# A gated DeltaNet chunk inverse rewritten: diagonal blocks of 64 by 64 x 64 products, and a block step to join them

## The chip, the cores and the metric

The kernel runs on one NeuronCore of one Trainium2 chip (trn2). The metric is the device time of one execution in microseconds (us). Three executions of the kernel before took 2860.15, 2866.6 and 2876.06 us; their median is 2866.6 us. One further execution was profiled; its rows are what this document reads.

## The reference, cut to what matters

Two transformer blocks of two layers each run one after the other on 256 tokens of width 1024, all in float32. The first block ends each layer with a mixture of experts. The second block's first layer has a bidirectional gated DeltaNet, for the 256 context tokens and for the 256 latent tokens. Per chunk of tokens it solves a unit lower triangular system:

```python
m = jnp.where(strict, jnp.einsum('nbhik,nbhjk->nbhij', k_beta, kc) * decay, 0.0)
a = jnp.eye(C, dtype=f32) + m
u = lax.linalg.triangular_solve(a, v_beta, left_side=True, lower=True, unit_diagonal=True)
w = lax.linalg.triangular_solve(a, k_beta * jnp.exp(gcum)[..., None],
                                left_side=True, lower=True, unit_diagonal=True)
```

The reference takes chunks of 64 tokens. The kernel takes chunks of 128, whose result is the same, and builds the inverse of `a` outright.

## The kernel before, in words

There are two streams of work. The stream S (tile names begin with m) carries the latent tokens: first the whole first block, then the second. The stream T (tile names begin with f) carries the context tokens through the second block's first layer. T's steps are handed out among S's mixtures of experts as fill: each S mark allows T a number of units (`FILL`, 14 per mark in the last mixture), and each `yield` of T says how many units its step used. A priority scheduler then puts every instruction of both streams into one fixed order per engine. An engine runs its instructions in that order; a tensor-engine (PE) instruction that waits holds up all behind it.

`gdn` (L1255) runs the DeltaNet for 2 chunks of 128 tokens, 2 directions and 4 heads. A pair (direction, chunk) is called a unit here. T works its four units one after the other (`groups` of one); S works two groups of two units. For each group there are three steps.

- `prepare` (L1276) builds the matrices of a unit, each of 128 partitions by 4 heads by 128: U (the strictly triangular system, transposed), the decayed scores `at`, the decayed keys `kt`, and room for X and Z.
- `level` (L1303), called 7 times (L1380), doubles the size of the inverted diagonal blocks: 1 to 2, 2 to 4, and so on to 128. X is the inverse so far, Z its transpose. Per level and unit there are up to three products (4 heads each, 128 x 128 by 128 x 128): pV = U'X, masked on VectorE (DVE) to the blocks of this level (L1311); pZ = V'Z (L1316); pX = Z'V (L1324). DVE then subtracts pX from X (L1325) and pZ from Z (L1326). Level 0 has no pX and the last level neither, so a unit takes 19 products and 20 DVE operations of 128 x 512 elements.
- `solve` (L1331) reads the state, multiplies by Z and updates output and state.

The hardware runs a float32 matmul as two instructions, so that a product of 4 heads is 8 MATMUL and 8 LDWEIGHTS in the trace. (The scheduler's order shows 4.)

Around `gdn` in each stream lie the projections before it, the 31-tap convolution `conv31` (L1083, mostly DVE at L1095, with a side chain on POOL), the output projection, and the feed-forward layers (tiles `mgu`, `fgu`, `facc`), which fill the gaps in PE's order. The tile `pada` (L997) is a modulation product from weights `adaw` loaded in threes; its matmuls stand among T's in PE's order. After the last mixture of experts comes a branch for experts that overflow (L911 and L912). It isn't taken.

Of the kernel before, what the change touches and what calls it, by code (L numbers as in the profile page):

```python
# [9 lines left out]
F32 = mybir.dt.float32  # L10
F32R = mybir.dt.float32r
BF = mybir.dt.bfloat16
I32 = mybir.dt.int32
AF = mybir.ActivationFunctionType
OP = mybir.AluOpType
# [328 lines left out]
class Kernel:  # L344
# [601 lines left out]
    def second_consts(self, S):  # L946
        nc, I, c = self.nc, self.I, self.consts
        self.gstrict = c.tile([128, 2, 128], F32, name="gstrict")
        self.gincl = c.tile([128, 2, 128], F32, name="gincl")
        nc.sync.dma_start(self.gstrict, I["c_gstrict"])  # L950
        nc.sync.dma_start(self.gincl, I["c_gincl"])
        self.gneg = c.tile([128, 2, 128], BF, name="gneg")
        gz = S.tmp([128, 2, 128], name="gz")
        nc.sync.dma_start(gz, I["c_gneg"])
        nc.vector.tensor_copy(self.gneg, gz)
        self.glev = c.tile([128, 2, 7, 128], BF, name="glev")
        for d in range(2):
            for q, n in ((0, 4), (4, 3)):
                gl = S.tmp([128, 4, 128], name="gl")
                nc.sync.dma_start(gl[:, :n], I["c_glev"][:, d, q:q + n])  # L960
                nc.vector.tensor_copy(self.glev[:, d, q:q + n], gl[:, :n])

        def row(name, src, n):
            t = c.tile([128, n], F32, name=name)
            nc.sync.dma_start(t, src[None, :].to_broadcast([128, n]))
            return t

        self.qkvw = c.tile([128, 12, 5], F32, name="qkvw")
        nc.sync.dma_start(self.qkvw, I["qkvw"])
        self.cfw = c.tile([128, 4, 31], F32, name="cfw")  # L970
        nc.sync.dma_start(self.cfw, I["cfw"])
        nc.vector.tensor_scalar(self.cfw, self.cfw, 0.5, None, op0=OP.mult)
        self.cfb = c.tile([128, 4], F32, name="cfb")
        nc.sync.dma_start(self.cfb, I["cfb"])
        self.onorm = row("onorm", I["gdn_out_norm_2"], 128)
        self.dtb = row("dtb", I["gdn_dt_bias_2"], 8)
        self.nega = row("nega", I["gdn_a_log_2"], 8)
        nc.scalar.activation(self.nega, self.nega, AF.Exp)
        nc.vector.tensor_scalar(self.nega, self.nega, -1.0, None, op0=OP.mult)
# [273 lines left out]
    def gdn(self, S, g, beta, krow, vrow, TT, ST, G, groups, first, need_state):  # L1253


        nc = self.nc
        V = nc.vector
        qT, kT = TT
        scale = 128.0 ** -0.5
        o = S.slab([128, 2, 4, 128], F32, "o")  # L1260
# [8 lines left out]
        egs = S.sm([128, 2, 2, 4], F32, "g_egs", 1)  # L1269
        V.tensor_scalar(egs, eg[:, 0], scale, None, op0=OP.mult)  # L1270
        yield 2.0
        idb = self.ident[:, None, :].to_broadcast([128, 4, 128])

        def bc(a):
            return a[:, :, None].to_broadcast([128, 4, 128])

        def prepare(d, c, i, kts):
            cs = slice(c * 128, (c + 1) * 128)
            A, B = G(), G()
            U, X, Z, at, kt = A[:, 0], A[:, 1], B[:, 0], B[:, 1], kts[:, i]  # L1280
            V.tensor_tensor(X, self.gstrict[:, d, None, :].to_broadcast([128, 4, 128]),
                            bc(g[:, c, 4 * d:4 * d + 4]), op=OP.mult)
            pd = S.ps([128, 4, 128], name="pD")
            for h in range(4):
                nc.tensor.matmul(pd[:, h], X[:, h], self.gincl[:, d], start=True, stop=False)
                nc.tensor.matmul(pd[:, h], self.identb, self.gneg[:, d], start=False, stop=True)
            E = S.tmp([128, 4, 128], name="E")
            nc.scalar.activation(E, pd, AF.Exp)
            p = S.ps([128, 4, 128], name="pkk")
            for h in range(4):  # L1290
                nc.tensor.matmul(p[:, h], kT[:, h, cs], kT[:, h, cs], start=True, stop=True)
            for h in range(4):
                V.scalar_tensor_tensor(U[:, h], p[:, h], beta[:, c, 4 * d + h:4 * d + h + 1], E[:, h],
                                       op0=OP.mult, op1=OP.mult)
            p = S.ps([128, 4, 128], name="pkq")
            for h in range(4):
                nc.tensor.matmul(p[:, h], kT[:, h, cs], qT[:, h, cs], start=True, stop=True)
            V.scalar_tensor_tensor(at, p, scale, E, op0=OP.mult, op1=OP.mult)
            last = 127 if d == 0 else 0
            V.tensor_tensor(kt, krow[:, c], E[:, :, last:last + 1].to_broadcast([128, 4, 128]), op=OP.mult)  # L1300
            return U, X, Z, at, kt

        def level(lev, batch):  # L1303

            V_ = []
            for (d, c), (U, X, Z, at, kt) in batch:
                pv = S.ps([128, 4, 128], name="pV")
                for h in range(4):
                    nc.tensor.matmul(pv[:, h], U[:, h], self.ident if lev == 0 else X[:, h], start=True, stop=True)
                v = S.tmp([128, 4, 128], name="Voff")  # L1310
                V.tensor_tensor(v, pv, self.glev[:, d, lev, None, :].to_broadcast([128, 4, 128]), op=OP.mult)  # L1311
                V_.append(v)
            for v, ((d, c), (U, X, Z, at, kt)) in zip(V_, batch):
                pz = S.ps([128, 4, 128], name="pZ")
                for h in range(4):
                    nc.tensor.matmul(pz[:, h], v[:, h], self.ident if lev == 0 else Z[:, h], start=True, stop=True)  # L1316
                if lev == 0:
                    V.tensor_tensor(X, idb, v, op=OP.subtract)
                    V.tensor_tensor(Z, idb, pz, op=OP.subtract)
                    continue  # L1320
                if lev < 6:
                    px = S.ps([128, 4, 128], name="pX")
                    for h in range(4):
                        nc.tensor.matmul(px[:, h], Z[:, h], v[:, h], start=True, stop=True)  # L1324
                    V.tensor_tensor(X, X, px, op=OP.subtract)  # L1325
                V.tensor_tensor(Z, Z, pz, op=OP.subtract)  # L1326

        done, seen = set(), set()

# [46 lines left out]
        for grp in groups:  # L1376
            kts = G()
            batch = [((d, c), prepare(d, c, i, kts)) for i, (d, c) in enumerate(grp)]
            yield 3.0 * len(grp)
            for lev in range(7):  # L1380
                level(lev, batch)
                yield 2.6 * len(grp)
            for (d, c), w in batch:
                solve(d, c, *w)
                yield 4.3
# [147 lines left out]
def prepare(x):  # L1533

    f = {k: np.asarray(v) for k, v in x.items()}
    o = {}
    c = np.ascontiguousarray
# [19 lines left out]
    q = f["w_q_up"].reshape(L, 3, 128, 8, 96)  # L1557
    q = np.concatenate([q, q[..., 80:96], q[..., 64:80]], -1)
# [37 lines left out]
    i = np.arange(128)  # L1596
# [17 lines left out]
    i, j = i[:, None], i[None, :]  # L1614
# [1 line left out]
    o["c_gincl"] = c(np.stack([i <= j, i >= j], 1).astype(f32))  # L1616
    o["c_gneg"] = c(np.stack([np.where(i <= j, 0, -30000.0), np.where(i >= j, 0, -30000.0)], 1).astype(f32))
    lev = []
    for s in range(7):
        w = 1 << s  # L1620
        lev.append(((i // (2 * w) == j // (2 * w)) & (i // w > j // w)).astype(f32))
    lev = np.stack(lev, 1)
    o["c_glev"] = c(np.stack([lev, lev.transpose(2, 1, 0)], 1))
    row = np.repeat(np.arange(4, dtype=f32), 64)
    col = np.tile(np.arange(64, dtype=f32), 4)
    inv = f32(10000.0) ** (-np.arange(32, dtype=f32) / f32(32))
# [125 lines left out]
```

## Time and profile before

| | |
|---|---|
| median of 3 runs | 2866.6 us (2860.15 to 2876.06) |
| the profiled execution's own time | 2867.61 us |
| its span in the trace | 2865.9 us |
| mean granted TensorE clock over the span | 0.972 |
| PE busy | 2663.8 us (93%) |
| DVE busy | 1663.0 us (58%) |
| ACT busy | 1009.6 us (35%) |
| POOL busy | 157.6 us (5%) |

How to read it: busy times are sums over the whole span, in which stages with different limits follow each other. The span in the trace is 1.7 us shorter than the execution's own time. A granted clock of 1.00 is 2.4 GHz and 0.50 is 1.2 GHz; a number between is a mean over the stretch.

### The profile page before, as it was taken

To read this page: it belongs to the slowest core of one execution; us is meant where nothing else is said; L and a number is where in the kernel's file an instruction comes from. 1 tells how busy PE (TensorE), PEld (TensorE's weight loads), DVE (VectorE), ACT (ScalarE), POOL (GpSimd) and SP (SyncE) were. 2 spreads that over 40 slices of the span, in tenths; PEclk is the share of its full clock that TensorE was granted. 3 is DMA by queue.
4 is the path that set the end of the run, shared out by engine and by line. 5 is a ranking of instruction groups with operands and counts; after the bars stand their busy time and mean duration, and the time that the engine had idled before them with its cause. 6 is when DMAs were issued, how large, how long until landed. Compare 5 with 4: busy or idle time off the path is not lost.

```text
span 2865.9 us, 44849 instructions
## 1 busy us (share of the span) xinstructions
PE 2663.8 (93%) x18016; PEld 2162.0 (75%) x18017; DVE 1663.0 (58%) x2895; ACT 1009.6 (35%) x1716; POOL 157.6 (5%) x183
## 2 busy tenths in 40 slices
PE   7999999888899998899999988999999999988998
PEld 6775555567755555788989986998989798965897
DVE  4752222548743474677687998734464434467766
ACT  3532223334533331123455213422333232244443
POOL 0000000010000120000000110000000000010000
PEclk9999999999999999999999999999999999999999
DMA  7659999873489997526655205654335743231564
GB/s 263 220 183 365 384 381 368 313 275 121 156 309 369 361 366 275 192 97 218 187 184 156 74 9 168 199 201 143 100 132 193 250 135 100 84 119 63 183 185 159
DMA packets 175720, 590.25 MB, mean 206 GB/s; under 512 B 29568, under 2 KB 32144, under 8 KB 175504
## 3 DMA queue, kind: packets, MB, share of 16 engines
q1 hardware_dynamic: 153504, 512.16, 51.3%
q10 hardware_dynamic: 18288, 66.59, 6.8%
q0 software_dynamic: 3712, 8.54, 0.9%
q8 instruction: 144, 2.36, 0.3%
q14 instruction: 72, 0.59, 0.1%
HBM read 572.39 MB, written 14.97 MB: 205 GB/s over the span
## 4 chain that ended last, share of the span: by engine, by line
PE 48%; DVE 6%; DMA 3%; issue 2%; POOL 1%; ACT 1%; SPq 0%; POOLq 0%; DVEq 0%; ACTq 0%
PE mgu L110 6%; PE mgu L111 6%; PE mgu L112 6%; PE macc L112 3%; PE macc L110 3%; PE macc L111 3%; PE fgu L111 3%; PE fgu L110 3%; PE fgu L112 3%; DMA adaw<-in_ada_w_dram 2%; PE facc L111 1%; PE facc L112 1%; PE facc L110 1%; PE pada L1035 1%; DVE mwl L104 1%
## 5 line engine op out<-in xcount | busy, mean ns | idle before, releaser
L104 DVE TENSOR_TENSOR mwl<-mraw,mwh 128x1024 fp32r<-128x1024 f32 x369 | 450.3, 1221 | 377.1 <-ACT mwh L103 376.7
L103 ACT ACTIVATE mwh<-mraw 128x1024 fp32r<-128x1024 f32 x369 | 390.8, 1059 | 695.4 <-PE mgu L111 151.9
L110 PE MATMUL mgu<-mxTh,mwh 128*128 128x256 f32 x1408 | 401.2, 285 | 2.6 <-ACT mxTh L170 2.6
L111 PE MATMUL mgu<-mxTl,mwh 128*128 128x256 f32 x1408 | 400.5, 285 | 2.4 <-DVE mxTl L171 2.3
L112 PE MATMUL mgu<-mxTh,mwl 128*128 128x256 f32 x1408 | 399.7, 284 | 0.0
L110 PEld LDWEIGHTS mgu<-mxTh,mwh 128*128 128x128 f32 x1408 | 270.1, 192 | 11.3 <-issue 4.4
L104 DVE TENSOR_TENSOR fwl<-fraw,fwh 128x1024 fp32r<-128x1024 f32 x127 | 154.1, 1220 | 210.0 <-ACT fwh L103 166.5
L111 PEld LDWEIGHTS mgu<-mxTl,mwh 128*128 128x128 f32 x1408 | 270.5, 192 | 3.7 <-DVE mxTl L171 3.4
L112 PEld LDWEIGHTS mgu<-mxTh,mwl 128*128 128x128 f32 x1408 | 270.4, 192 | 0.0
L807 PE MATMUL mpgu<-mraw,mxg 128*64 128x512 f32 x1024 | 239.4, 607 | 10.2 <-DMA mraw<-in_w_gu_dram 7.3
L103 ACT ACTIVATE fwh<-fraw 128x1024 fp32r<-128x1024 f32 x127 | 133.5, 1057 | 203.7 <-PE fgu L111 106.2
L807 PEld LDWEIGHTS mpgu<-mraw,mxg 128*64 128x64 f32 x1024 | 72.2, 139 | 136.4 <-issue 129.1
L111 PE MATMUL fgu<-fxTl,mwh 128*128 128x256 f32 x576 | 163.0, 283 | 0.0
L112 PE MATMUL fgu<-fxTh,mwl 128*128 128x256 f32 x576 | 162.7, 282 | 0.0
L110 PE MATMUL fgu<-fxTh,mwh 128*128 128x256 f32 x576 | 161.5, 280 | 0.0
L110 PE MATMUL fgu<-fxTh,fwh 128*128 128x256 f32 x480 | 140.7, 294 | 2.7 <-DVE fa L298 1.4
L112 PE MATMUL fgu<-fxTh,fwl 128*128 128x256 f32 x480 | 138.7, 291 | 4.0 <-DVE fwl L104 4.0
L111 PE MATMUL macc<-mwl,macth 128*128 128x512 f32 x352 | 138.3, 393 | 1.1 <-DVE mwl L104 1.1
L110 PE MATMUL macc<-mwh,macth 128*128 128x512 f32 x352 | 138.7, 394 | 0.0
L111 PE MATMUL fgu<-fxTl,fwh 128*128 128x256 f32 x480 | 138.0, 290 | 0.0
L112 PE MATMUL macc<-mwh,mactl 128*128 128x512 f32 x352 | 137.9, 393 | 0.0
L835 PE MATMUL mpd<-mraw,mea 128*64 128x512 f32 x512 | 119.5, 598 | 0.5 <-DMA mraw<-in_w_down_dram 0.3
(611 smaller groups left out, 5657.3 us busy)
## 6 DMA issues: line engine op xcount, KB each, us to landing
mraw<-in_w_gu_dram SPq DMA_DIRECT2D x256, 512.0 KB, 8.3
mraw<-in_ffn_gu_dram SPq DMA_DIRECT2D x176, 512.0 KB, 4.5
adaw<-in_ada_w_dram SPq DMA_DIRECT2D x144, 512.0 KB, 6.1
mraw<-in_w_down_dram SPq DMA_DIRECT2D x128, 512.0 KB, 9.5
mraw<-in_ffn_dn_dram SPq DMA_DIRECT2D x88, 512.0 KB, 4.1
fraw<-in_ffn_gu_dram ACTq DMA_DIRECT2D x60, 512.0 KB, 5.1
fraw<-in_ffn_dn_dram ACTq DMA_DIRECT2D x30, 512.0 KB, 6.1
mraw<-in_w_in_dram SPq DMA_DIRECT2D x26, 512.0 KB, 5.3
```

The lines of the kernel that those rows point to most:

```text
L103: nc.scalar.activation(h[:, :m], raw[:, o:o + m], AF.Copy)
L104: nc.vector.tensor_tensor(l[:, :m], raw[:, o:o + m], h.bitcast(F32)[:, :m], op=OP.subtract)
L110: self.kb.latest = nc.tensor.matmul(ps, a[0], b[0], start=start, stop=False)
L111: nc.tensor.matmul(ps, a[0], b[1], start=False, stop=False)
L112: nc.tensor.matmul(ps, a[1], b[0], start=False, stop=stop)
L807: return nc.tensor.matmul(p[64 * g:64 * g + 64], xg(k), raw, start=k == 0, stop=k == 7)
L835: return nc.tensor.matmul(acc[64 * c:64 * c + 64], at[:, f], raw, start=f == 0, stop=f == 3)
L1035: m = nc.tensor.matmul(p[32 * g:32 * g + 2], self.cond[:, k], raw[:, g * 256:(g + 1) * 256], start=k == 0, stop=k == 7)
```

## The change

The first six levels now invert only the two diagonal blocks of 64 of each unit. X and the transposed inverse lie side by side in the two 64-column halves of one tile (XZ), the two diagonal blocks above each other in the partitions. A product of 4 heads is 8 matmuls of 64 x 64 by 64 x 64 (`half_mm`), whose operands and outputs lie in partitions 0 to 63 for one block and 64 to 127 for the other, alternating; both write the same PSUM tile. DVE operations on them have 128 x 256 elements in place of 128 x 512. The seventh level is replaced by `join`: one off-diagonal 64 x 64 block per head by two products of 4 matmuls each, a DVE copy, a DVE multiplication by -1 and two ACT copies that put the diagonal blocks into the full Z, which POOL has set to zero in `prepare`. The masks shrink from 7 levels of 128 columns to 6 of 64. The units that T's steps report shrink too (1.8 for 2.6 per level, 1.5 for the join).

```diff
@@ second_consts
-        self.glev = c.tile([128, 2, 7, 128], BF, name="glev")
+        self.glev = c.tile([128, 2, 6, 64], BF, name="glev")
...
+        self.identh = c.tile([128, 64], F32, name="identh")
+        for b in range(2):
+            nc.vector.tensor_copy(self.identh[64 * b:64 * b + 64], self.ident[64 * b:64 * b + 64, 64 * b:64 * b + 64])
@@ gdn
-        idb = self.ident[:, None, :].to_broadcast([128, 4, 128])
+        idb = self.identh[:, None, :].to_broadcast([128, 4, 64])
@@ prepare
             U, X, Z, at, kt = A[:, 0], A[:, 1], B[:, 0], B[:, 1], kts[:, i]
+            nc.gpsimd.memset(Z, 0.0)
@@
+        halves = [slice(0, 64), slice(64, 128)]
+
+        def half_mm(p, a, b):
+
+            for h in range(4):
+                for s in halves:
+                    nc.tensor.matmul(p[s, h], a(h, s), b(h, s), start=True, stop=True)
+
         def level(lev, batch):
...
-            for (d, c), (U, X, Z, at, kt) in batch:
-                pv = S.ps([128, 4, 128], name="pV")
-                for h in range(4):
-                    nc.tensor.matmul(pv[:, h], U[:, h], self.ident if lev == 0 else X[:, h], start=True, stop=True)
-                v = S.tmp([128, 4, 128], name="Voff")
-                V.tensor_tensor(v, pv, self.glev[:, d, lev, None, :].to_broadcast([128, 4, 128]), op=OP.mult)
+            for (d, c), (U, XZ, Z, at, kt) in batch:
+                X = XZ[:, :, 0:64]
+                pv = S.ps([128, 4, 64], name="pV")
+                half_mm(pv, lambda h, s: U[s, h, s], lambda h, s: self.identh[s] if lev == 0 else X[s, h])
+                v = S.tmp([128, 4, 64], name="Voff")
+                V.tensor_tensor(v, pv, self.glev[:, d, lev, None, :].to_broadcast([128, 4, 64]), op=OP.mult)
                 V_.append(v)
...
-                if lev < 6:
-                    px = S.ps([128, 4, 128], name="pX")
-                    for h in range(4):
-                        nc.tensor.matmul(px[:, h], Z[:, h], v[:, h], start=True, stop=True)
-                    V.tensor_tensor(X, X, px, op=OP.subtract)
-                V.tensor_tensor(Z, Z, pz, op=OP.subtract)
+                px = S.ps([128, 4, 64], name="pX")
+                half_mm(px, lambda h, s: Zc[s, h], lambda h, s: v[s, h])
+                V.tensor_tensor(X, X, px, op=OP.subtract)
+                V.tensor_tensor(Zc, Zc, pz, op=OP.subtract)
+
+        def join(batch):
+
+            V_ = []
+            for (d, c), (U, XZ, Z, at, kt) in batch:
+                near, far = halves if d == 0 else halves[::-1]
+                p = S.ps([128, 4, 64], name="pV")
+                for h in range(4):
+                    nc.tensor.matmul(p[far, h], U[near, h, far], XZ[near, h, 0:64], start=True, stop=True)
+                v = S.tmp([128, 4, 64], name="Voff")
+                V.tensor_copy(v[far], p[far])
+                for s in halves:
+                    nc.scalar.activation(Z[s, :, s], XZ[s, :, 64:128], AF.Copy)
+                V_.append(v)
+            for v, ((d, c), (U, XZ, Z, at, kt)) in zip(V_, batch):
+                near, far = halves if d == 0 else halves[::-1]
+                p = S.ps([128, 4, 64], name="pZ")
+                for h in range(4):
+                    nc.tensor.matmul(p[near, h], v[far, h], XZ[far, h, 64:128], start=True, stop=True)
+                V.tensor_scalar(Z[near, :, far], p[near], -1.0, None, op0=OP.mult)
@@ the loop over groups
-            for lev in range(7):
+            for lev in range(6):
                 level(lev, batch)
-                yield 2.6 * len(grp)
+                yield 1.8 * len(grp)
+            join(batch)
+            yield 1.5 * len(grp)
```

The scheduler's order changes with it. On PE, in the first group of S's DeltaNet, a level of two units was this (mpV, mpZ, mpX are the PSUM tiles of the three products):

```order
L1309 MATMUL mpV<-mG 128x128 x8
L1316 MATMUL mpZ<-mG,mVoff 128x128 x4
L1324 MATMUL mpX<-mVoff,mG 128x128 x4
L1316 MATMUL mpZ<-mG,mVoff 128x128 x4
L1324 MATMUL mpX<-mVoff,mG 128x128 x4
```

and is now, with the same order of products and twice the matmuls, each of a quarter of the array:

```order
L1312 MATMUL mpV<-mG 64x64 x16
L1312 MATMUL mpZ<-mG,mVoff 64x64 x8
L1312 MATMUL mpX<-mVoff,mG 64x64 x8
L1312 MATMUL mpZ<-mG,mVoff 64x64 x8
L1312 MATMUL mpX<-mVoff,mG 64x64 x8
```

The second place is PE at the end of the last mixture of experts (mpgu, mpgT and mpd are the products of its last two experts), ahead of the branch L912. Before, with T's second unit (tiles f) beginning there:

```order
L835 MATMUL mpd<-mraw,mea 64x512 x8
L1309 MATMUL fpV<-ident,fG 128x128 x4
L1297 MATMUL fpkq<-fqkvT 128x128 x2
L1316 MATMUL fpZ<-ident,fVoff 128x128 x4
L1309 MATMUL fpV<-fG 128x128 x4
L997 MATMUL pada<-adaw,cond 2x256 x5
L911 TENSOR_LOAD mo_ci
```

and now:

```order
L1312 MATMUL fpZ<-fG,fVoff 64x64 x5
L835 MATMUL mpd<-mraw,mea 64x512 x8
L820 MATMUL mpgT<-ident,mgsb 128x128 x4
L1312 MATMUL fpZ<-fG,fVoff 64x64 x3
L1312 MATMUL fpX<-fVoff,fG 64x64 x8
L1312 MATMUL fpV<-fG 64x64 x8
L835 MATMUL mpd<-mraw,mea 64x512 x8
L1312 MATMUL fpZ<-fG,fVoff 64x64 x8
L1312 MATMUL fpX<-fVoff,fG 64x64 x8
L1312 MATMUL fpV<-fG 64x64 x8
L1312 MATMUL fpZ<-fG,fVoff 64x64 x8
L1312 MATMUL fpX<-fVoff,fG 64x64 x7
```

Before, T's second unit stood at its level 1 at the branch. Now it stands near the end of its level 4, and products of its levels 1 and 2 stand ahead of the last experts' products. The third place is DVE in the same S group (mcw is the convolution's accumulator). Before, from one mask to the next:

```order
L1311 TENSOR_TENSOR mVoff<-mpV,glev 128x512 x2
L1095 SCALAR_TENSOR_TENSOR mcw<-mu,cfw,mcw 128x249
L1095 SCALAR_TENSOR_TENSOR mcw<-mu,cfw,mcw 128x250
L1095 SCALAR_TENSOR_TENSOR mcw<-mu,cfw,mcw 128x251
L1325 TENSOR_TENSOR mG<-mG,mpX 128x512
L1326 TENSOR_TENSOR mG<-mG,mpZ 128x512
L1095 SCALAR_TENSOR_TENSOR mcw<-mu,cfw,mcw 128x252
L1325 TENSOR_TENSOR mG<-mG,mpX 128x512
L1326 TENSOR_TENSOR mG<-mG,mpZ 128x512
```

and now:

```order
L1323 TENSOR_TENSOR mVoff<-mpV,glev 128x256 x2
L1097 SCALAR_TENSOR_TENSOR mcw<-mu,cfw,mcw 128x246
L1097 SCALAR_TENSOR_TENSOR mcw<-mu,cfw,mcw 128x247
L1335 TENSOR_TENSOR mG<-mG,mpX 128x4x64
L1336 TENSOR_TENSOR mG<-mG,mpZ 128x4x64
L1097 SCALAR_TENSOR_TENSOR mcw<-mu,cfw,mcw 128x248
L1335 TENSOR_TENSOR mG<-mG,mpX 128x4x64
L1336 TENSOR_TENSOR mG<-mG,mpZ 128x4x64
```

One convolution step less stands in a level, and more of the convolution stands behind the last level.

## Rows read from the trace of the kernel before

**Rows 1.** The page: busy us of each engine (share of the span) xinstructions.

```profile
PE 2663.8 (93%) x18016; PEld 2162.0 (75%) x18017; DVE 1663.0 (58%) x2895; ACT 1009.6 (35%) x1716; POOL 157.6 (5%) x183
```

**Rows 2.** Windows: stretch in us, its length, busy of each engine, clock, DMA share, GB/s.

```profile
1130.00:1168.00 38.00, 26.86 (x180) 22.50 (x180) 26.03 (x40) 8.62 (x15) 2.04 (x2) 0.78 0.65 227
1168.00:1272.00 104.00, 99.65 (x893) 92.19 (x892) 66.50 (x114) 21.09 (x34) 5.31 (x6) 1.00 0.45 146
1598.00:1650.00 52.00, 48.09 (x401) 45.65 (x400) 50.18 (x95) 7.80 (x15) 6.79 (x9) 1.00 0.11 34
1650.00:1668.00 18.00, 11.93 (x88) 11.24 (x87) 16.32 (x32) 3.61 (x7) 4.59 (x6) 0.91 0.04 15
1668.00:1715.00 47.00, 44.19 (x356) 41.91 (x353) 43.84 (x80) 3.70 (x7) 5.14 (x7) 0.96 0.02 7
```

**Rows 3.** Timeline, S's DeltaNet: start us, us, engine line op out<-in xcount [idle before <-releaser].

```profile
1608.00 1.95 PE L1309 MATMUL mpV<-ident,mG 128*128 128x128 f32 x16
1611.81 1.87 PEld L1309 LDWEIGHTS mpV<-mG 128*128 128x128 f32 x16
1616.62 0.68 DVE L1325 TENSOR_TENSOR mG<-mG,mpX 128x512 f32<-128x512 f32 x1
1617.21 0.67 DVE L1326 TENSOR_TENSOR mG<-mG,mpZ 128x512 f32<-128x512 f32 x1
1623.87 1.06 PE L1309 MATMUL mpV<-mG 128*128 128x128 f32 x8
1630.17 2.10 PE L1309 MATMUL mpV<-mG 128*128 128x128 f32 x16
1646.13 1.06 PE L1338 MATMUL mpkS<-fstate,mqkvT 128*128 128x128 f32 x8
```

**Rows 4.** Groups by line, 1590 to 1745 us: busy, mean ns | idle before, releaser.

```profile
L1095 DVE SCALAR_TENSOR_TENSOR mcw<-mu,cfw,mcw 128x247 f32<-128x247 f32 (+14 forms) x86 | 43.0, 500 | 1.5
L1311 DVE TENSOR_TENSOR mVoff<-mpV,glev 128x512 f32<-128x512 f32 x28 | 19.2, 687 | 1.3 <-PE mpV L1309 0.6
```

**Rows 5.** Timeline of DVE: an operation of 128x256 and the next one.

```profile
1599.49 0.42 DVE L1236 SCALAR_TENSOR_TENSOR mu<-mgth,mpj 128x256 f32<-128x256 f32 x1
1599.82 0.47 DVE L1095 SCALAR_TENSOR_TENSOR mcw<-mu,cfw,mcw 128x247 f32<-128x247 f32 x1
```

**Rows 6.** Timeline: matmuls with 64 stationary columns, outputs in alternating partition halves.

```profile
109.34 0.42 PEld L625 LDWEIGHTS mpo<-mpTs,mv 128*64 128x64 f32 x8 [0.27 <-ACT mpTs L621]
109.34 0.66 PE L625 MATMUL mpo<-mpTs,mv 128*64 128x128 f32 x8
```

**Rows 7.** The instructions on tile mpo: duration ns min/median/max, first to last start, forms.

```profile
L625 PEld LDWEIGHTS mpo<-mpTs,mv x96: 132/137/231, 109.3 to 723.9; 128*64 128x64 f32 x96
L625 PE MATMUL mpo<-mpTs,mv x96: 272/273/476, 109.3 to 724.0; 128*64 128x128 f32 x96
```

**Rows 8.** The page: the experts' products, halves alternating, 512 moving columns.

```profile
L807 PE MATMUL mpgu<-mraw,mxg 128*64 128x512 f32 x1024 | 239.4, 607 | 10.2 <-DMA mraw<-in_w_gu_dram 7.3 <-issue 2.3 <-ACT mxg L774 0.4
```

**Rows 9.** Windows, tile mpaux alone (64 stationary, 2 moving columns, one half): PE, PEld, DVE.

```profile
212.50:213.50 1.00, 1.00 (x21) 1.00 (x19) 0.00 (x0) 1.00 0.92 336
...
214.50:215.50 1.00, 1.00 (x13) 1.00 (x12) 0.00 (x0) 0.52 0.99 348
```

**Rows 10.** Timeline of PE, end of the last mixture and T's second unit.

```profile
1109.07 1.06 PE L1368 MATMUL fpS<-fG 128*128 128x128 f32 x8
1110.05 3.65 PE L835 MATMUL mpd<-mraw,mea 128*64 128x512 f32 x16
1126.90 1.04 PE L997 MATMUL pada<-adaw,cond 128*2 128x256 f32 x14 [0.30 <-PEq L912]
1163.60 1.89 PE L997 MATMUL pada<-adaw,cond 128*2 128x256 f32 x16 [1.80 <-DMA adaw<-in_ada_w_dram]
1167.90 0.36 PE L112 MATMUL mgu<-mxTh,mwl 128*128 128x256 f32 x1
```

More of the change, by code (lines that the diff above doesn't have):

```diff
@@ L955, in second_consts @@
         nc.vector.tensor_copy(self.gneg, gz)
-        self.glev = c.tile([128, 2, 7, 128], BF, name="glev")
+        self.glev = c.tile([128, 2, 6, 64], BF, name="glev")
         for d in range(2):
[L958 to L961, printed above, removed]
+            gl = S.tmp([128, 6, 64], name="gl")
+            nc.sync.dma_start(gl, I["c_glev"][:, d])
+            nc.vector.tensor_copy(self.glev[:, d], gl)
+        self.identh = c.tile([128, 64], F32, name="identh")
+        for b in range(2):
+            nc.vector.tensor_copy(self.identh[64 * b:64 * b + 64], self.ident[64 * b:64 * b + 64, 64 * b:64 * b + 64])
         def row(name, src, n):
@@ L1312, in level @@
                 V_.append(v)
-            for v, ((d, c), (U, X, Z, at, kt)) in zip(V_, batch):
-                pz = S.ps([128, 4, 128], name="pZ")
-                for h in range(4):
-                    nc.tensor.matmul(pz[:, h], v[:, h], self.ident if lev == 0 else Z[:, h], start=True, stop=True)
+            for v, ((d, c), (U, XZ, Z, at, kt)) in zip(V_, batch):
+                X, Zc = XZ[:, :, 0:64], XZ[:, :, 64:128]
+                pz = S.ps([128, 4, 64], name="pZ")
+                half_mm(pz, lambda h, s: v[s, h], lambda h, s: self.identh[s] if lev == 0 else Zc[s, h])
@@ L1317, in level @@
                 if lev == 0:
                     V.tensor_tensor(X, idb, v, op=OP.subtract)
-                    V.tensor_tensor(Z, idb, pz, op=OP.subtract)
+                    V.tensor_tensor(Zc, idb, pz, op=OP.subtract)
                     continue
-                if lev < 6:
-                    px = S.ps([128, 4, 128], name="pX")
-                    for h in range(4):
-                        nc.tensor.matmul(px[:, h], Z[:, h], v[:, h], start=True, stop=True)
-                    V.tensor_tensor(X, X, px, op=OP.subtract)
@@ L1326, in level @@
-                V.tensor_tensor(Z, Z, pz, op=OP.subtract)
+                px = S.ps([128, 4, 64], name="pX")
[14 more added lines that the diff above has]
+                V_.append(v)
+            for v, ((d, c), (U, XZ, Z, at, kt)) in zip(V_, batch):
+                near, far = halves if d == 0 else halves[::-1]
[3 more added lines that the diff above has]
+                V.tensor_scalar(Z[near, :, far], p[near], -1.0, None, op0=OP.mult)
@@ L1618, in prepare @@
     lev = []
-    for s in range(7):
+    i, j = np.arange(64)[:, None], np.arange(64)[None, :]
+    for s in range(6):
         w = 1 << s
@@ L1622, in prepare @@
     lev = np.stack(lev, 1)
-    o["c_glev"] = c(np.stack([lev, lev.transpose(2, 1, 0)], 1))
+    lev = np.stack([lev, lev.transpose(2, 1, 0)], 1)
+    o["c_glev"] = c(np.concatenate([lev, lev]))
     row = np.repeat(np.arange(4, dtype=f32), 64)
```

## The prediction

> **What bounds the kernel now.** Read the page first: PE is busy 93% of the span and DVE 58% [rows 1]. That is an average, so the table of windows comes next, for the stretches in which the changed products run [rows 2]. T's DeltaNet lies beside the end of the last mixture of experts and the start of S's feed-forward layer. From 1130 to 1168 us PE is busy 26.9 of 38 us, since it waits for T's chain and for weights. From 1168 to 1272 us it is busy 99.7 of 104: there T's products compete with S's mgu, and every us of PE work removed is worth nearly a us. S's DeltaNet stands alone on its path from 1598 to 1715 us, and there DVE is the fuller engine: 50.2 of 52, 16.3 of 18, 43.8 of 47 us, with PE at 48.1, 11.9 and 44.2. So two engines are near their limit there, and both must be relieved. The groups by line say what fills DVE: 43.0 us of the convolution beside the level operations, 28 masks at 687 ns among them [rows 4]. The timeline gives the rhythm: the first group's levels begin at 1608.0 and its solve at 1646.1, 38.1 us, and a full level of two units takes 6.3 us (1623.87 to 1630.17) [rows 3].
>
> **PE, per unit.** Before: 16 weight loads of 128 columns start over 1.87 - 0.19 us, 0.112 us apart [rows 3]; a product is 8 of them, 0.9 us, and 19 products make 17.0 us. After: 17 products of 16 instructions each, and a join of 16 instructions, each product of it in one quarter of the array. Their pace p is the unknown, since nothing in the trace uses half the rows and half the columns. It is bounded by three neighbours. The expert products, in alternating column halves, take 239.4/1024 = 0.234 us per 512 columns [rows 8]; 128 columns alone take 0.112, which is 0.45 for 512, so that two halves do run side by side, into one PSUM tile. In proportion 64 columns would take 0.112/2/2 = 0.028 us: the lower end. The nearest row in size is mpo, 64 stationary columns in alternating halves: its loads start (0.42 - 0.137)/7 = 0.040 us apart and its matmuls, twice as long as the new ones, (0.66 - 0.273)/7 = 0.055 [rows 6, 7]. And mpaux, 64 stationary and 2 moving columns always in one half, issues 20 pairs in a us, 0.050 each, at full clock [rows 9]. I take 0.040, the load pace of mpo, because with moving columns halved the loads come to the front; 0.028 and 0.055 are the ends. A unit is then 17 x 16 x p + 16 x 0.050 = 272p + 0.8 = 11.7 us (8.4 to 15.8), a gain of 5.3 us.
>
> **DVE, per unit.** Two subtractions of 128x512 start 0.59 us apart [rows 3], a 128x256 operation and its successor 0.33 [rows 5]. 20 x 0.6 = 12.0 us become 18 x 0.33 + 2 x 0.33 = 6.6, so 5.4 us less; four units in S make 21.6.
>
> **S's DeltaNet.** A level of two units is 6 products: 48 x 0.112 = 5.4 us, and 6.3 in the trace, so 0.9 us of waits. After: 96p + 0.9 = 4.7 us at p = 0.040. A group is level 0 (4 products and waits, 3.5 us), five levels (23.5) and a join (1.6 of PE and some 1.4 of DVE in between), 30 us for 38.1: 8 us each, 16 for both. DVE sets a limit of its own: with the idle shares of [rows 2] kept, it allows its 21.6 us. The convolution now ends behind the levels, so I count **-17 us** (p = 0.028: levels of 3.6 us, where DVE's limit of -21 decides; 0.055: levels of 6.2, a group 38.3, 0).
>
> **T's DeltaNet.** Behind the branch at 1126.9 us [rows 10] stand before: 16 products of unit two (14.3 us) and units three and four (34.0), 48.3 us of PE. The order after has 3 products and a join of unit two there and the same two units: 3 x 16p + 0.8 + 2 x (272p + 0.8) = 592p + 2.4 = 26.1 us. That is 22.2 less: partly cheaper products, partly work moved ahead of the branch, where PE waits for expert weights. Two costs go against it. First, quarter-array products alternate with S's full-array mgu. Row fpS to mpd shows such a switch: the eighth fpS starts at 1109.07 + 7 x 0.112 = 1109.85 and mpd at 1110.05, 0.20 later and not 0.11, so 0.09 us each [rows 10]; four per level over twelve levels are 4.3 us. Second, T's levels 1 and 2 now stand ahead of the last experts' products, whose chain (product, mask, product, subtraction) costs them some 3 us that the weights' arrival doesn't cover. Net **-15 us** (0.028: 48.3 - 19.0 - 7.3 = -22; 0.055: 48.3 - 35.0 - 7.3 = -6). PE's idle time there, for adaw weights above all (1.8 us before one pada [rows 10]), I take as unchanged.
>
> The Trainium skill, TensorEngine Tiling (Array Packing), section Tiling Modes, says that a change of tiling mode drains the engine; the 0.09 us agree in direction, and it gives no price.
>
> Nothing is counted for the rest, with its cover: POOL's memset of Z (needed only by the join, six levels later; uncovered, one POOL step of the convolution's chain); the two ACT copies (beside the join's products; uncovered, under 1 us per unit); smaller masks at the start.
>
> **Sum.** 2867.6 (the profiled execution's own time, 1.0 above the median) - 17 - 15 = 2835.6, forecast **2835 us**, 1.1% faster. Changes under 0.5% (14 us) can't be told from none here.
>
> **Rivals.**
> - *The halves run fully side by side* (p = 0.028): 2867.6 - 21 - 22 = 2825. For it: the experts' 0.234 us. Against: those have eight times the columns behind each load.
> - *The halves don't overlap* (p = 0.055 or so): 2867.6 - 0 - 6 = 2862, no change. For it: every row with overlap uses all 128 rows, none shows two row halves side by side; 16 instructions of half the length then take what 8 took. The Trainium skill, TensorEngine Tiling (Array Packing), section Restrictions and Gotchas, speaks for this one: "Different row tiles cannot access same PSUM bank simultaneously". No run here shows it yet; the rows have column halves sharing a PSUM tile, at full overlap.
> - *The clock falls, and the kernel is slower.* The mpaux stretch has PE busy throughout, and yet the granted clock goes from 1.00 to 0.52, between the levels of 2.4 and 1.2 GHz, and the pace from 20 to 12.5 pairs per us, 0.080 us each [rows 9]. Quarter-array products keep PE busy with little work too, and in S's levels nothing else runs beside them. At p = 0.080 a level of two units is 8.6 us, a group 52 (+14 each, +28), and T's PE work behind the branch 49.8, with 7.3 of switches and delay +9: 2867.6 + 37 = 2905. It decides from p = 0.058, where S's two groups (544p + 8.4 us each, for 38.1) and T's 592p + 9.7 (for 48.3) together break even. Against it: 64 moving columns are far more than 2, and S's mgu runs among T's products.
> - *T's moved work holds the experts up*: if the last expert products wait 15 us rather than 3, and T's gain is gone, 2850; if S's convolution becomes the end of its stage as well, 2862.
>
> **Chances.** Forecast (p 0.034 to 0.047) 0.42; full overlap 0.20; no overlap 0.20; clock 0.12; hold-up 0.06. Faster by over 0.5% (under 2853): the first two, half of the hold-up, and a third of the no-overlap case, with p under 0.050: 0.72. Slower: 0.12. Same: 0.16. The range reaches from 2815, a little below full overlap since idle may close too, to 2864, and leaves out the clock and the tails.
>
> **What would show it.** Right: LDWEIGHTS and MATMUL of mpZ at 64x64 start about 0.04 us apart; full levels of S take 4.7 us; DVE's 128x256 masks last 0.42 us; the granted clock stays above 0.9 from 1598 us on; S's first uninterrupted mgu comes no later than 1168 us; T's last product comes well before 1272. Wrong: a pace of 0.055 or more, a clock near 0.5 in the levels or mpd of the last expert late behind T's products. If levels shrink as forecast and the time doesn't, the convolution on DVE, or pada's wait for adaw, took their place.

## The result and the profile after

Four runs of the changed kernel took 2827.94 to 2838.48 us, median 2831.64; four of the kernel before 2857.8 to 2876.06, median 2863.38. The ratio on record is 0.9879, 95% interval [0.9859, 0.9898] (the two medians as they stand give 0.9889): **1.2% faster**, where 2835 was forecast. The profiled execution after took 2827.94 us of its own, the lowest of its four, so that the two traces differ by 39.7 us and the medians by 31.7. The page after, for [rows 1]:

```profile
PE 2614.7 (93%) x19104; PEld 2105.0 (74%) x19105; DVE 1619.5 (57%) x2895; ACT 1017.0 (36%) x1732; POOL 164.0 (6%) x191
```

Two stretches hold the change. Both are cut at the same instructions in both traces. The *T stretch* goes from the 925th mpgu matmul (near the end of the last mixture) to the 409th macc matmul (S's first feed-forward layer behind it); T's DeltaNet lies in it. The *S stage* goes from the last mpj (S's projections ahead of its DeltaNet) to the 545th macc matmul, the 41st behind S's DeltaNet. The expectations below call its end the first macc; that one comes about 10 us earlier in every run (1744.3 before, 1707.4 after). Windows, columns as in [rows 2] (PE, PEld, DVE, ACT, POOL); before:

```profile
1050.50:1446.90 396.40, 365.29 (x2564) 305.92 (x2561) 255.05 (x387) 118.35 (x171) 20.54 (x23) 0.96 0.61 207
1596.40:1754.30 157.90, 135.99 (x1006) 125.33 (x1005) 142.91 (x263) 26.82 (x45) 19.28 (x24) 0.97 0.16 51
```

and after:

```profile
1056.10:1424.50 368.40, 339.56 (x3058) 275.53 (x3055) 235.46 (x387) 121.98 (x180) 23.75 (x28) 0.97 0.66 222
1575.80:1718.00 142.20, 117.40 (x1596) 103.72 (x1595) 130.07 (x273) 33.75 (x58) 20.00 (x26) 0.94 0.23 75
```

The T stretch lost 28.0 us, and PE's busy time there 25.7. The S stage lost 15.7, and DVE's busy time there 12.8; PE lost 18.6 and its idle time grew. That points to PE for the first; what bounds the second is taken up below. Together the two lost 43.7 us and the span 40.1, so that the other stretches grew by 3.6. Such differences lie within those of single traces: T's first fpV, ahead of which the change touches little but the masks, starts at 1032.5 to 1040.6 us in the profiled runs of this study.

The S stage didn't hold the same work before and after. T's feed-forward product facc (PE) has twice the matmuls in it; the tile facc alone, before and after:

```profile
1596.40:1754.30 157.90, 11.88 (x46) 8.26 (x46) 0.68 (x1) 0.00 (x0) 0.97 0.16 51
1575.80:1718.00 142.20, 24.22 (x92) 17.92 (x92) 2.05 (x3) 0.00 (x0) 0.94 0.23 75
```

The rhythm in S's first group, PE, for [rows 3]:

```profile
1591.70 0.63 PE L1312 MATMUL mpX<-mVoff,mG 64*64 64x64 f32 x16
1592.17 0.63 PE L1312 MATMUL mpZ<-mG,mVoff 64*64 64x64 f32 x16
1592.63 0.63 PE L1312 MATMUL mpX<-mVoff,mG 64*64 64x64 f32 x16
...
1601.91 0.68 PE L1312 MATMUL mpV<-mG 64*64 64x64 f32 x16 [0.27 <-DVE mG L1335]
...
1605.41 0.68 PE L1312 MATMUL mpV<-mG 64*64 64x64 f32 x16 [0.28 <-DVE mG L1335]
...
1610.75 1.16 PE L1368 MATMUL mpkS<-fstate,mqkvT 128*128 128x128 f32 x8
```

Products of 16 instructions start 0.467 us apart: **0.029 us per instruction**. A level of two units takes 3.5 us (1601.91 to 1605.41; 6.3 before), the group 23.6 (first mpV at 1587.11; 38.1 before). DVE beside it, for [rows 4, 5], at the 0.33 us pace that [rows 5] had promised:

```profile
1599.50 0.98 DVE L1097 SCALAR_TENSOR_TENSOR mcw<-mu,cfw,mcw 128x246 f32<-128x246 f32 x2
1600.40 0.41 DVE L1335 TENSOR_TENSOR mG<-mG,mpX 128x256 f32<-128x256 f32 x1
1600.73 0.42 DVE L1336 TENSOR_TENSOR mG<-mG,mpZ 128x256 f32<-128x256 f32 x1
```

But behind the last mpat (1677.16; the last product of S's solve) DVE still has eleven convolution steps to do, mixed with T's feed-forward (fa, factl, fwl):

```profile
1681.64 0.42 DVE L298 TENSOR_TENSOR fa<-fa,fgu 128x256 f32<-128x256 f32 x1
1681.97 0.99 DVE L1097 SCALAR_TENSOR_TENSOR mcw<-mu,cfw,mcw 128x251 f32<-128x251 f32 x2
1682.88 0.42 DVE L301 TENSOR_TENSOR factl<-fa,facth 128x256 fp32r<-128x256 f32 x1
1683.22 1.99 DVE L1097 SCALAR_TENSOR_TENSOR mcw<-mu,cfw,mcw 128x247 f32<-128x247 f32 x4
1685.22 1.22 DVE L104 TENSOR_TENSOR fwl<-fraw,fwh 128x1024 fp32r<-128x1024 f32 x1
```

The mtp that needs the convolution (mtp transposes the outputs of DeltaNet and convolution) starts at 1705.9: 27.9 us from the last mpat matmul's start (1678.0), 17.0 before (1725.0 to 1742.0). This distance, before and after:

```profile
1725.00:1742.00 17.00, 11.02 (x52) 8.24 (x51) 15.14 (x29) 5.73 (x10) 2.76 (x3) 1.00 0.51 186
1678.00:1705.90 27.90, 23.79 (x99) 18.04 (x99) 25.93 (x47) 9.64 (x13) 2.76 (x3) 0.94 0.35 102
```

S's solve ends 26.4 us earlier after the last mpj, and 10.9 of that are given back here, with 10.8 more of DVE's busy time: 5.0 us are the convolution's, 4.9 are T's fwl (6 for 2).

The end of the last mixture, PE, for [rows 10]:

```profile
1111.89 0.68 PE L1312 MATMUL fpV<-fG 64*64 64x64 f32 x16 [0.88 <-DVE fG L1330]
1113.60 0.90 PE L1312 MATMUL fpZ<-fG,fVoff 64*64 64x64 f32 x10 [1.03 <-DVE fVoff L1323]
1114.43 6.26 PE L807 MATMUL mpgu<-mraw,mxg 128*64 128x512 f32 x16
...
1123.74 3.65 PE L835 MATMUL mpd<-mraw,mea 128*64 128x512 f32 x16
...
1130.42 3.65 PE L835 MATMUL mpd<-mraw,mea 128*64 128x512 f32 x16 [0.31 <-DVE mea L825]
```

The last mpd starts 13.4 us later than before (1116.99), 7.9 of it since the 925th mpgu. T's products, which wait for DVE, stand ahead of the last experts, and the last mpgu runs at a fallen clock.

### The profile page after: what moved, and what is told of

Its sections match the earlier page's. It is cut to its first block, busy times and chain, and to the rows that moved or that the text cites. A ratio compares the mean times of both kernels' runs of the same rounds, so it can differ in the third digit from the quotient of the medians.

```text
span 2825.8 us, 47068 instructions
## 1 busy us (share of the span) xinstructions
PE 2614.7 (93%) x19104; PEld 2105.0 (74%) x19105; DVE 1619.5 (57%) x2895; ACT 1017.0 (36%) x1732; POOL 164.0 (6%) x191
```

## The experiments

All ratios are to runs of the kernel before on the same chip; stretch and stage are from one trace each.

| kernel | median us | ratio [95%] | T stretch | S stage |
|---|---|---|---|---|
| before | 2863.4 | 1 | 396.4 | 157.9 |
| the change | 2831.6 | 0.9879 [0.9859, 0.9898] | 368.4 | 142.2 |
| e1_halves_in_turn | 2839.0 | 0.9899 [0.9869, 0.9929] | 372.0 | 146.0 |
| e9_long_runs | 2846.2 | 0.9928 [0.9908, 0.9948] | 385.0 | 148.2 |
| e2_unit_two_held | 2828.4 | 0.9871 [0.9851, 0.9891] | 364.0 | 142.7 |
| e3_taps_to_pool | 2821.8 | 0.9849 [0.9829, 0.9870] | 375.0 | 132.4 |
| e10_13_taps_not_held | 2819.4 | 0.9835 [0.9815, 0.9854] | 373.0 | 132.1 |
| e5_held_13_taps | 2823.0 | 0.9846 [0.9825, 0.9867] | 369.8 | 136.2 |
| e6_held_16_taps | 2820.5 | 0.9835 [0.9812, 0.9858] | 368.2 | 134.4 |
| e7_t_alone | 2844.5 | 0.9923 [0.9898, 0.9948] | 371.5 | 157.8 |
| e4_s_alone | 2859.2 | 0.9974 [0.9960, 0.9987] | 396.8 | 142.7 |
| e8_s_alone_same_masks | 2854.9 | 0.9946 [0.9922, 0.9970] | 397.0 | 142.3 |

**Why 0.029? First, the halves in turn** (e1):

```diff
-            for h in range(4):
-                for s in halves:
+            for s in halves:
+                for h in range(4):
```

> The changed kernel, with the two halves of a product in turn: all four heads of the upper 64 partitions, then all four of the lower, in place of alternating. In the changed kernel a product of 16 instructions takes 0.467 us, 0.029 per instruction. Theory: neighbouring instructions on different halves run side by side, so without alternation a product takes 0.85 to 0.9 us, a full level of two units in S goes from 3.5 to about 6 us, S's stage loses 20 to 30 us and T's 8 to 15, total 2855 to 2875 us. Rival: an instruction of 64 x 64 costs 0.029 us by its size, whatever stands beside it: product 0.47 us, total 2828 to 2838 us.

Neither number came: the total is 1 us above the rival's range, and its interval overlaps the change's. The weight loads tell why:

```profile
1593.73 0.19 PEld L1312 LDWEIGHTS mpX<-mVoff,mG 64*64 64x64 f32 x2
1593.79 0.14 PEld L1312 LDWEIGHTS mpZ<-mG,mVoff 64*64 64x64 f32 x1
1593.84 0.14 PEld L1312 LDWEIGHTS mpX<-mVoff,mG 64*64 64x64 f32 x1
1593.84 0.14 PEld L1312 LDWEIGHTS mpZ<-mG,mVoff 64*64 64x64 f32 x1
1593.90 0.54 PEld L1312 LDWEIGHTS mpX<-mVoff,mG 64*64 64x64 f32 x11
```

The first loads of mpX, on the upper half, start among the last of mpZ, on the lower. Then mpX is alone: its 11 loads start (0.54 - 0.14)/10 = 0.040 apart on average, since they include its own change of halves; inside a half it is 0.05 to 0.06. Products start 0.57 us apart (mpX at 1593.73, the next mpZ at 1594.30). When mpX's first matmul starts, three of mpZ's last eight, which stand ahead of it in PE's order, are still to start (1593.78, 1593.84, 1593.90), and so runs of 8 overlap in part. Runs too long for that settle it (e9):

```diff
+        def half_mms(jobs):
+            for s in halves:
+                for p, a, b in jobs:
+                    for h in range(4):
+                        nc.tensor.matmul(p[s, h], a(h, s), b(h, s), start=True, stop=True)
...
-                half_mm(pz, lambda h, s: v[s, h], lambda h, s: self.identh[s] if lev == 0 else Zc[s, h])
...
-                half_mm(px, lambda h, s: Zc[s, h], lambda h, s: v[s, h])
...
+            half_mms(jobs)
```

> The changed kernel with longer runs on one half: first the upper half of all products that are ready together (pV of both units of S, then pZ and pX of both), then the lower half; 16 to 32 instructions in a run where e1 had 8. In e1 the instructions of one half start 0.055 us apart, but some 6 of the next half's start beside the last ones, so that a product took 0.577 us. Theory (two halves run side by side only where neighbouring instructions in PE's order alternate, and a half alone takes 0.055 each): 0.045 us or more per instruction over a level, S's full level 5 to 5.5 us (3.5 in the changed kernel), S's stage 146 to 156 us (142.2), the stretch from 1050 us to S's macc 380 to 392 us (368.5), total 2848 to 2865 us. Rival (PE runs ahead through any run of instructions, or an instruction costs 0.029 by its size): total 2828 to 2840 us.

```profile
1601.70 0.54 PEld L1312 LDWEIGHTS mpZ<-mG,mVoff 64*64 64x64 f32 x8 [0.19 <-DVE mVoff L1324]
1602.16 0.54 PEld L1312 LDWEIGHTS mpX<-mVoff,mG 64*64 64x64 f32 x8
1602.63 0.54 PEld L1312 LDWEIGHTS mpZ<-mG,mVoff 64*64 64x64 f32 x8
```

```profile
1050.20:1435.20 385.00, 364.61 (x3058) 301.56 (x3055) 236.59 (x387) 122.18 (x180) 24.03 (x28) 0.95 0.63 212
1585.10:1733.30 148.20, 128.12 (x1551) 118.81 (x1550) 124.92 (x263) 30.50 (x55) 19.67 (x26) 0.94 0.17 55
```

Eight loads of one half take 0.46 us: 0.058 each. Over S's levels the mean step is 0.051 (0.029 in the change, 0.039 in e1), a level takes 4.9 us, and the total is 2846, 2 us under the expected range. The theory holds: **the overlap comes from alternating neighbours**, and without it some 60% of the gain remain in S (9.7 of 15.7 us) and 40% in T (11.4 of 28.0). PE's time in the T stretch rose by 25.1 us and the stretch by 16.6. In S PE's rose by 10.7, and the stage by only 6.0: slower products give DVE time for the convolution, and mtp comes 19.1 us after the last mpat, not 27.9. T's fill in the stage is again as before the change (46 facc matmuls, 13.5 us, for 24.2 in the change), so that S's own products rose by some 21 us.

**What bounds S's stage? Taps moved from DVE to POOL** (a tap is one step of the convolution; e3, both streams; e10, S alone):

```diff
-            if k < 16 or k % 2 == 0:
+            if k < 10 or k % 2 == 0:
```

> The changed kernel, with 6 of the 23 convolution taps per channel block that DVE does moved to the side chain on ACT and POOL, which then has 13 of them. 24 taps of 0.40 us in S's stage, 9.6 us of DVE, go. Theory (the convolution on DVE ends S's stage: 12 of its taps stand behind the last mpat, and 28.7 us pass from the last mpat to the next mtp, where 17.9 passed before the change): that distance falls to 18 to 22 us, total 6 to 10 us less, 2821 to 2826. Rival (T's feed-forward fill on PE and its fwl on DVE set that distance): distance and total as they were, 2829 to 2838. A third: 13 POOL steps of about 0.85 us and as many ACT copies, 11 us per block, become the end: total up.

> The changed kernel with 13 of S's taps per block on POOL, T's taps as they were and unit two not held. Theory (S's stage is DVE's; holding unit two only moves work): S's stage 132 to 136 us, the stretch from 1050 us to S's macc 367 to 371 us as in the changed kernel, total 2819 to 2825 us, as good as e5. Rival (the held unit is worth some us of its own): total 2826 to 2832.

The edit moves fewer taps than these texts say. Even taps stay on DVE whatever the bound, so that of taps 10 to 15 only 11 and 13 go (15 was never there): 2 per block and not 6, 9 per block on POOL and not 13. The traces have 84 steps on DVE for 92, and 36 additions on POOL for 28. Of the 8 that moved, 6 are in the S stage, 3.1 us of DVE. Windows of e10:

```profile
1051.40:1424.40 373.00, 343.00 (x3059) 278.24 (x3055) 235.72 (x387) 122.05 (x180) 23.75 (x28) 0.96 0.65 219
1574.60:1706.70 132.10, 107.16 (x1563) 95.59 (x1562) 119.93 (x258) 33.91 (x60) 25.81 (x32) 0.96 0.21 66
```

The stage fell from 142.2 to 132.1 us, DVE's busy time in it from 130.07 to 119.93, and PE's as much, from 117.40 to 107.16. S's products are the same in both. So the equal fall doesn't single out DVE, and most of it isn't the taps': of DVE's 10.1 us, 6.0 are six steps of T's fln and 2.4 two of T's fwl, which the new order puts behind the stage, and of PE's 10.2, 7.9 are T's facc (59 matmuls for 92). By parts, up to the last mpat's start in the change and in e10, and from there to the mtp in e10:

```profile
1575.80:1678.00 102.20, 81.52 (x1439) 75.49 (x1438) 92.34 (x213) 18.86 (x39) 17.24 (x23) 0.93 0.11 33
1574.50:1673.10 98.60, 79.19 (x1440) 73.42 (x1439) 92.61 (x211) 22.18 (x43) 23.04 (x29) 0.97 0.12 35
1673.10:1695.60 22.50, 16.98 (x72) 12.98 (x71) 20.40 (x41) 7.54 (x11) 2.77 (x3) 0.92 0.55 186
```

Up to the last mpat 3.6 us went with DVE's work unchanged, at a higher granted clock. From there to mtp 5.4 went (6.7 in e3, which takes 21.2), with 5.5 of DVE's work and 6.8 of PE's. DVE is the fuller engine there in both (25.9 of 27.9 us and 20.4 of 22.5), which speaks for DVE as the limit of this last part. Shown is that with these taps on POOL the stage and the total are shorter. That DVE ends the stage is argued, not shown: T's feed-forward changed its place with the taps on both engines, and no run moves one without the other. e10 has the lowest median of the study, 0.4% under the change (e6 has the same ratio); the T stretch came 2 us above its expected range. That e3 met its range is luck, since it was worked out from three times the taps; e10's range went by e3's trace.

**Did T's moved work cost anything? Unit two held back** (e2; lastz is 0 times the last expert's output):

```diff
         for i, grp in enumerate(groups):
+            if S.name == "f" and i == 1:
+                while self.at < sum(len(m) for m in self.marks.values()):
+                    yield 1e3
+                gl = S.sm([128, 2, 8], F32, "g_l", 1)
+                V.tensor_copy(gl, g)
+                V.tensor_scalar(gl[0:64], g[0:64], self.lastz, None, op0=OP.add)
+                g = gl
```

> The changed kernel, with T's second unit made to wait for the last expert's output (its decay input has 0 times that output added), so that no product of unit two stands among the last experts' products. Theory (T's moved work holds the experts up): the last mpgu takes 3.65 us and not 6.26, at full clock, the last mpd starts 8 to 14 us earlier (about 1118 to 1124 for 1130.4), the branch and S's first mgu as much earlier; of unit two's own PE time (about 9 us) half lies in gaps before the first mgu and half beside S's mgu, so that the total falls by 3 to 9 us, to 2822 to 2829. Rival (the work only changes its place, and T's later end costs what the experts gain): the last mpd earlier all the same, total 2829 to 2838 or above.

```profile
1096.76 7.09 PE L808 MATMUL mpgu<-mraw,mxg 128*64 128x512 f32 x32
1105.48 3.65 PE L836 MATMUL mpd<-mraw,mea 128*64 128x512 f32 x16 [1.63 <-DMA mraw<-in_w_down_dram]
...
1111.74 3.65 PE L836 MATMUL mpd<-mraw,mea 128*64 128x512 f32 x16 [1.92 <-DVE mea L826]
...
1143.41 0.50 PE L110 MATMUL mgu<-mxTh,mwh 128*128 128x256 f32 x2 [0.35 <-ACT mxTh L170]
```

The experts end as the theory says: last mpd at 1111.74 for 1130.42, first mgu at 1143.4 for 1174.9. Counted from the 925th mpgu, the first mgu comes after 91.3 us, for 118.8 in the change and 109.3 before. Yet the T stretch is only 4.4 us shorter, and the total, though at the upper end of the theory's range, can't be told from the change's (ratio 0.9871): T's products now lie beside mgu. e5 against e10, the same pair with the taps moved, gives 369.8 for 373.0 in the stretch, and a total that is higher, not lower. So the hold-up is real and large where one looks at the experts, and PE's work behind it takes most of it back, as the rival has it.

Both together, and with more taps (e5, e6; `first` is 10 and 4 for S, 16 for T, which makes 9 and 12 taps per block on POOL in S):

```diff
-            if k < 16 or k % 2 == 0:
+            if k < first or k % 2 == 0:
```

> Unit two held back as in e2, and 13 taps per block on POOL as in e3, but in S alone (T keeps 7). Theory (both hold: the held unit shortens the stretch from the last experts to the middle of S's first feed-forward layer, and S's DeltaNet stage is DVE's): S's stage, last mpj to first macc, 132 to 134 us as in e3 (142.2 in the changed kernel), T's moved end as in e2; total 2815 to 2821 us, ratio to before 0.982 to 0.985, under the changed kernel and under e2 and e3. Rival (one of the two gains was drift of a run): total as e3's, 2821.8, or above.

> As e5, with 16 taps per block on POOL in S and 14 on DVE: 12 more taps of 0.40 us leave DVE, 4.8 us. Theory (DVE still ends S's stage): its length falls by another 4 to 5 us to 127 to 129 us. Rival (PE's chain of products and masks or the chain ACT-POOL of 16 x 0.85 = 13.6 us per block is the next limit): 131 to 134 us, no gain or a loss against e5.

e5 missed its range by 2 us, and its S stage by 2: its rival holds. Its distance to mtp is e10's, 22.5; but up to the last mpat it took 102.7 us at a granted clock of 0.92, e10 98.6 at 0.97, with the same work on DVE (92.8 and 92.6). So two traces of this part can differ by 4 us with the same work on DVE. In e6 the convolution is out of the way (mtp comes 16.9 us after the last mpat, as before the change), but the solve itself got longer, 106.2 us: rival again. What bounds it then wasn't tried.

**Do the parts add up?** One stream alone (e4 and e8 with `old` for T, e7 for S):

```diff
+        old = S.name == "f"
...
-            for lev in range(6):
-                level(lev, batch)
+            for lev in range(7 if old else 6):
+                (level_old if old else level)(lev, batch)
```

> The new inverse in S alone; T keeps seven full levels. By the places where the two traces stand, S's stage gave about 15 us (157.9 us from its last mpj to the first macc before, 142.2 after) and T's about 22, some of it drift of the run. Theory (the two gains add up): about 15 us less than before, ratio 0.9935 to 0.996. Rival (S's stage is held by its convolution and by T's fill and gains little by itself, or T's part is worth nothing by itself): ratio over 0.998, or under 0.990.

> e4 again (new inverse in S alone), without loading a second set of masks: they are cut from the old table. In e4 S's stage was 15 us shorter and the total only 6. Theory (e4 lost 5 to 7 us by loading and rounding both mask tables at its start: its products stand 5.2 us late at 79 us and 7.3 us late at 142 us against before): now 13 to 16 us under before, ratio 0.9943 to 0.9957. Rival (S's gain is given back behind its stage): ratio 0.997 to 0.999 again, and the loss lies behind 1760 us.

> The new inverse in T alone; S keeps seven full levels. Its masks are cut from the old table by four small copies, so that no mask is loaded twice. Theory (the gains add: in the traces the stretch from expert 14's products near 1050 us to S's macc near 1447 us is 396.4 us before and 368.4 after): that stretch 366 to 372, S's stage 157 to 159 as before, ratio to before 0.989 to 0.992. Rival (T's earlier end is worth less in the total, since it only moves S's wait): stretch 380 or more, ratio over 0.994.

In e4 the S stage was as expected (142.7) and the total, 0.26% under before, was short of it. The first mpq of e4, and of e8 behind it, 79.4 us before:

```profile
L110 PE MATMUL mpq<-mqlh,mwh x48: 279/283/472, 84.7 to 685.9; 128*128 128x256 f32 x48
```

```profile
L110 PE MATMUL mpq<-mqlh,mwh x48: 279/283/467, 81.3 to 682.3; 128*128 128x256 f32 x48
```

Loading two sets of masks cost e4 some 3 to 5 us at its start (7.3 late at 142 us, e8 2.0, other runs up to 3.8), and e8 gained 0.54%, in its range. e7 gained 0.77%, a shade less than expected, with stretch and stage as expected. Together 1.31%, the change 1.21%: the parts add. The intervals of e4 and e8 overlap, so that e4's loss is explained in size only roughly.

## Why the prediction was right

**Total and direction** held: by the medians -31.7 us, for -32. The two terms missed in opposite ways: S -15.7 for -17, T -28.0 for -15 in the one trace (23 to 28 over e10, e7 and the change). By medians, one stream alone gave 0.54% (S, e8) and 0.77% (T, e7), some 15 and 22 us. In the pair of traces the two sum to -43.7, which is the sum of the first rival (-43) and not the forecast's. So that the number came within 4 us is in part luck: T's term was too small, and single executions differ by more than that.

**The pace.** The step that failed is "I take 0.040, the load pace of mpo, because with moving columns halved the loads come to the front". It is 0.029. And mpo's loads had no steady pace of 0.040: that is the mean over a row of eight. Taken one by one in the trace, they start in pairs, two within 0.007 us; the second pair follows the first after 0.055, the third and fourth after 0.108 each, which is 0.054 per load and the pace of its matmuls. The new loads of the two halves start in pairs too, two within 0.007 us and the next two 0.058 later, so that loads overlap too. The first rival (0.028) had the pace right. The second, no overlap, had the pace of what it supposed: e9 shows it, 0.051 to 0.058. Its price was too high, 2862 for e9's 2846, since it gave S nothing and e9's S stage gained 9.7 us. The Trainium skill, TensorEngine Tiling (Array Packing), section Restrictions and Gotchas, spoke for that rival. For these quarters, which alternate between two row halves and write two partition halves of one PSUM tile, the runs contradict it, if one PSUM tile lies in one bank: 0.029 alternating, twice that on one half at a time (0.058 in e9).

**S.** With 0.029 the prediction's own sum said levels of 3.6 us and -21, with DVE's limit deciding. Levels took 3.5, and DVE's time on the inverse fell as computed: masks and subtractions of the levels above 0 (the masks of level 0 with them), 19.2 + 16.3 + 13.6 us before, took 9.7 + 8.3 + 8.3 after. That the stage gave only 15.7 is the step "the convolution now ends behind the levels, so I count -17". It came near by luck: it was counted by a pace that was wrong, and what took the rest is the 10.9 us behind the last mpat. Half of that is the convolution, which the step named and didn't price; the other half is T's feed-forward, which no term had (in the whole stage 7 fwl of 1.22 us for 4, and 46 more facc matmuls).

**T.** 592p + 2.4 is 19.6 at 0.029, which with 7.3 of costs gives -21, the rival's -22; the mis-sized pace is half of the miss. The rest, 2 to 7 us, isn't accounted for term by term: the sum began at the branch, and cheaper products of units one and two ahead of it lie in the stretch too. The hold-up was 7.9 us at the last mpd and 9.5 at the first mgu, which came at 1174.9 and not "no later than 1168"; in the stretch, e2 and e5 put it at 3 to 4 us, the 3 of the sum. The switch between products was sized about right; a visit of one T product among mgu:

```profile
1214.01 0.28 PE L111 MATMUL mgu<-mxTl,mwh 128*128 128x256 f32 x1
1214.22 0.68 PE L1312 MATMUL fpV<-fG 64*64 64x64 f32 x16
1214.83 0.39 PE L112 MATMUL mgu<-mxTh,mwl 128*128 128x256 f32 x1
```

From mgu to mgu 0.82 us, less 0.12 for the mgu and 0.467 for the product: 0.23 for two switches, where 2 x 0.09 were counted. T's last fpS starts at 1238.3 (1271.6 before).

**The other rivals.** The clock's fall as the main effect didn't come: 1.00 from 1575.8 to 1610.7, S's first group, and 0.94 over the stage (0.97 before). From 1628 to 1680 us it was 0.87, under the 0.9 that the prediction took for a sign of being right. The hold-up rival came true in its mechanism at the experts and in S's convolution, and in its price at neither.

## What to carry to other kernels

When a product is cut into quarter-array pieces, issue them alternating between the two halves: here neighbours overlapped fully (0.029 us each), runs of 16 and more hardly (0.051). Before pricing a faster product, ask which engine ends the stage, and what other work the new order will put there: here PE's gain counted in full only in T, and in S half of what came back behind the levels was T's. Two busy times that fall alike don't prove a cause: count the instructions that moved, and those that only changed their place. Work that moves ahead of a wait may delay that wait by many us and still cost little (here 8 to 10 us late, at 3 to 4), if the work has to be done on the same engine anyway; compare the whole stretch, not the late instruction.

## What was not expected of the hardware

The clock fell behind a spell of waiting. In the changed kernel PE was busy 2.76 of 5 us while T's small products waited for DVE, and the last mpgu then ran at the level of 1.2 GHz, 6.26 us for 3.65 (the kernel before has a fall there too: 0.70 from 1100 to 1105 us, behind 5 us with PE busy for 3.05):

```profile
1110.00:1115.00 5.00, 2.76 (x44) 2.12 (x46) 4.68 (x7) 1.34 (x2) 0.00 (x0) 0.79 0.58 231
1115.00:1120.00 5.00, 5.00 (x14) 1.39 (x12) 0.00 (x0) 0.77 (x1) 0.00 (x0) 0.53 0.00 0
```

And a convolution step on DVE takes longer while POOL adds beside it. POOL's seven additions from 1592.58 to 1598.60 cover the first row, and not the second:

```profile
1595.19 1.80 DVE L1097 SCALAR_TENSOR_TENSOR mcw<-mu,cfw,mcw 128x243 f32<-128x243 f32 x2
...
1602.98 0.98 DVE L1097 SCALAR_TENSOR_TENSOR mcw<-mu,cfw,mcw 128x249 f32<-128x249 f32 x2
```

Over the S stage of the change the 14 steps that meet a POOL addition take 0.65 us on average, the other 63 take 0.47. The 14 meet ACT's copies for POOL as well; but 12 of the others meet some ACT instruction and no POOL, and take 0.47 too. So a tap on POOL is not quite free for DVE, one reason why e6's last step brought little; that it is the whole reason isn't shown.
